# Bursts that end in 128 columns, and a load slot held at the start: a hybrid decoder layer on one core

## The chip, the core and the metric

The kernel runs on one NeuronCore of a Trainium2 chip. The metric is the device time of one launch in microseconds (us), the median over the runs; smaller is better. Profiles are of one execution each. TensorE (PE, its weight loads PEld) multiplies, VectorE (DVE) and ScalarE (ACT) work elementwise, GpSimd (POOL) does small work, SyncE (SP) issues most of the DMAs. A wait is a semaphore that another engine or a DMA raises.

## What is computed

One layer of a decoder on 256 tokens of 2048 channels, in float32:

```python
h = rmsnorm(x, g_mix)
u_pool, q, k, v, q_idx, k_idx, w_idx = split(h @ w_in)
pool_out = pool_mixer(u_pool, w_pool, pool_scale)    # trailing means of 2, 4, 8, 16 tokens
attn_out = dsa_attention(q, k, v, q_idx, k_idx, w_idx, rel_bias)
    # 16 index heads score the causal keys, the best 64 stay; 8 heads of 128 attend
x = x + concat(pool_out, attn_out) @ w_out
x = x + conv_ffn(rmsnorm(x, g_ffn), w_up, conv_w, conv_b, w_down)   # 2048 -> 2 x 5632 -> 2048
x = x + (p @ w_ple_proj) * sigmoid(rmsnorm(x, g_ple) @ w_ple_gate)
return rmsnorm(x, g_final)
```

## The kernel before

Every weight comes through `unit` (L74): a DMA of up to 552 KB on SP into a raw tile of the pool `wraw`, which has four slots; then ACT casts it to a high part (L87, type float32r) and DVE subtracts that from the raw tile, which gives the low part (L88). The raw slot is free when DVE is through. The two parts stand in one of three w tiles. Activations are kept the same way, high and low beside each other.

A product is therefore made of several on TensorE. `cm_matmul` (L143), by far the most frequent, takes each 128 x 128 block of weights twice: the high part against high and low activations, 512 columns (L147), and the low part against the high activations, 256 columns (L148). This pair is most of the kernel: query, key and pool projections, the output projection, the up- and down-projections of the ConvFFN. `tm_matmul` (L167) has the activations as the stationary operand and makes three products for each block (L174, L175, L176).

The stages follow each other in this order. First the input stage (`with ExitStack() as c1`). Its loop over 16 K tiles (L227) multiplies values and index keys: a K tile is 1104 columns of weights, which K tile 0 loads in two units of 368 and 736 columns; six products are made for each of three thirds, 18 a tile. Ahead of the loads stand those of xT, one K tile (128 KB) or two (256 KB) at a time (L230); the first K tile of x comes with the parameters (L93). Then come the pairs for the index queries, q and k, and the pool group, and between them, in bursts, other products: `score` (L305, index scores, float32r, 128 and 256 columns for the two token blocks), the relative bias (L338), `logits` (L388, plain float32, two passes each), the transposes of the softmax (L434 to L436), `attend` (L440, plain float32), and the pool maps (L483). After that the output projection (`out_unit`, L514), the ConvFFN (L535 on), the embedding stage (L584 on) and the stores.

No order is written out by hand. The program is traced, a planner with its own model of times then orders the instructions of each engine, and waits are added where data or a slot need them. A load whose slot isn't free by the planner's times lets later instructions of SP past it, and a burst of other products can land between any two instructions of a pair. `in_order` keeps a few DMAs at their places. At most eight of SP's DMAs are under way: each further one also waits for the landing of the eighth before it. `rstd_rows` (L136) puts four passes of 128 columns (L139) just ahead of the ConvFFN's pairs.

Of the kernel before, what the change touches and what calls it, by code (L numbers as in the profile page):

```python
# [10 lines left out]
F32 = mybir.dt.float32  # L11
# [7 lines left out]
P = 128  # L19
S = 256  # L20
# [14 lines left out]
UNIT = 3 * NVK  # L35
# [15 lines left out]
def layer(ctx: ExitStack, tc: tile.TileContext, a: dict):  # L51
    nc = tc.nc
    in_order = tc.keep_in_program_order
    V, A, T, G = nc.vector, nc.scalar, nc.tensor, nc.gpsimd
# [11 lines left out]
    wraw = ctx.enter_context(tc.tile_pool(name="wraw", bufs=4))  # L66
# [2 lines left out]
    acc = ctx.enter_context(tc.tile_pool(name="acc", bufs=4, space=PSUM))  # L69
    aux = ctx.enter_context(tc.tile_pool(name="aux", bufs=4, space=PSUM))  # L70

    n_units = 0

    def unit(src, n=1024, keep=None, at=(0, LOW)):  # L74

        nonlocal n_units
        raw = wraw.tile([P, UNIT], F32, name="raw")
        nc.sync.dma_start(raw[:, :n], src)
        if keep:
            hi = keep.tile([P, n], F32R, name="hi", bufs=5)  # L80
            lo = keep.tile([P, n], F32R, name="lo", bufs=5)
        else:
            w = wsp[n_units % 3].tile([P, SLOT], F32R, name="w")
            n_units += 1
            h0, l0 = at if n <= 1024 else (0, UNIT)
            hi, lo = w[:, h0:h0 + n], w[:, l0:l0 + n]
        A.copy(hi, raw[:, :n])  # L87
        V.tensor_sub(lo, raw[:, :n], hi.bitcast(F32))  # L88
        return hi, lo
# [117 lines left out]
    with ExitStack() as c1:  # L207
# [8 lines left out]
        qk = ar.tile([P, 2 * NH, S], F32, name="qk", tag="qkA")  # L216
# [10 lines left out]
        for kt in range(KT):  # L227
            if kt == 1 or (kt and kt % 2 == 0):
                k1 = kt + 1 if kt == 1 else kt + 2
                nc.sync.dma_start(xt[:, kt:k1, :], a["xT"][:, kt:k1, :])  # L230
            cuts = (0, NVK, 3 * NVK) if kt == 0 else (0, 3 * NVK)
            ws = [unit(a["w_first"][kt][:, c0:c1], c1 - c0) for c0, c1 in zip(cuts, cuts[1:])]
            split(hT[:, kt, :S], hT[:, kt, S:],
                  xt[:, kt, :] if kt else prm[:, C_CONV:],
                  prm[:, C_GMIX + kt:C_GMIX + kt + 1])
            for n in range(3):
                i = sum(n * NVK >= c for c in cuts) - 1
                tm_matmul(pvk[n], *ws[i], hT, (kt,), kt == 0, kt == KT - 1, n=NVK,
                          w0=n * NVK - cuts[i])
            if kt == 3:  # L240
                in_order(nc.sync.dma_start(ident, a["ident"]))
            if kt == 5:
                in_order(nc.sync.dma_start(xt[:, 0:1, :], a["xT"][:, 0:1, :]))
            if kt >= 7 and kt < 15:
                square(kt - 7)
# [59 lines left out]
        def score(j, qr):  # L305
            pds = [aux.tile([P, 512], F32, name="ps") for _ in range(2)]
            for e in range(2):
                for t, (o, n) in enumerate(((0, P), (P, S))):
                    q = qr[:, e, t * P:(t + 1) * P]
                    T.matmul(pds[e][:, o:o + n], q, kr[:, :n], start=True, stop=False)  # L310
                    T.matmul(pds[e][:, o:o + n], q, kr[:, S:S + n], start=False, stop=True)  # L311
            for e in range(2):
                h = 2 * j + e
                rl = ar.tile([P, 384], F32, name="rl", bufs=2)
                A.activation(rl, pds[e][:, :384], AF.Relu, scale=1.0 / 32.0)
                for t in range(2):
                    src = s0[t] if h == 0 else sc[t]
                    V.scalar_tensor_tensor(sc[t], rl[:, :P] if t == 0 else rl[:, P:],
                                           wx[:, t, h:h + 1], src, op0=OP.mult, op1=OP.add)
# [68 lines left out]
        def logits(t, h0):  # L388
            n = P * (t + 1)
            hb = 512 // n  # L390
            pl = aux.tile([P, 512], F32, name="ps")
            for h in range(h0, h0 + hb):
                T.matmul(pl[:, (h - h0) * n:(h - h0 + 1) * n],  # L393
                         qk[:, 2 * h, t * P:(t + 1) * P], qk[:, 2 * h + 1, :n],
                         start=True, stop=True)
            hs = slice(h0, h0 + hb)
            V.scalar_tensor_tensor(L[t][:, hs, :], pl.rearrange("p (h s) -> p h s", s=n), P ** -0.5,
                                   tb[:, hs, S - n:], op0=OP.mult, op1=OP.add)
# [22 lines left out]
        for j in range(12, 16):  # L421
            qk_tile(j)
            if j >= 14:
                h0 = 4 * (j - 14)
# [15 lines left out]
        def attend(h, pt):  # L440
            po = aux.tile([P, 512], F32, name="ps")
            for e in range(2):
                vs = slice((h + e) * P, (h + e + 1) * P)
                T.matmul(po[:, e * S:(e + 1) * S], v[:, 0, vs], pt[:, e, :S],  # L444
                         start=e == 0, stop=False, skip_group_check=True)
                T.matmul(po[:, e * S + P:(e + 1) * S], v[:, 1, vs], pt[:, e, S:],
                         start=False, stop=e == 1, skip_group_check=True)
            po2 = po.rearrange("p (e s) -> p e s", s=S)
            split(catA[:, h:h + 2, :S], catA[:, h:h + 2, S:], po2)
# [316 lines left out]
```

## Time and profile before

| | us |
|---|---|
| median of 3 runs | 1181.37 (1181.3 to 1181.61) |
| the profiled execution | 1181.5 |
| its span, first to last instruction | 1179.7 |
| TensorE busy in the span | 1168.7 |
| VectorE | 855.8 |
| ScalarE | 643.8 |
| GpSimd | 8.9 |

The input stage ends at about 265 us, the output projection at 357, the up-projection at 827 and the down-projection at 1066 us; the last product starts at 1169.7 us. In the rows below times are us from the span's start unless said otherwise. A matmul's row begins when TensorE takes it up; its end is modelled, so its length holds the way through the array too, and rows of neighbours overlap. What a product occupies TensorE for is read from start to start.

### The profile page before, as it was taken

Reading aid. Unit: us, or ns where it says so; the run is one execution under the profiler, and the core shown is the slowest. Engines: PE = TensorE matmul, PEld = TensorE weight load, DVE = VectorE, ACT = ScalarE, POOL = GpSimd, SP = SyncE. Lnnn points to the kernel's source line nnn. Section 1 sums busy time; section 2 is a strip of 40 time slices with the busy share of each in tenths; the row PEclk is TensorE's granted clock in tenths of the full one; section 3 lists DMA queues with packets and bytes.
Section 4 is the critical chain, followed back from the end, with each engine's and each line's share of the span. In section 5 each row is a group of like instructions: output and inputs, shape, how many; then the busy total and the mean of one; then the engine's idle time right before and its main releaser. Section 6 shows DMA issues by size and latency. Waiting matters only on the chain.

```text
span 1179.7 us, 17843 instructions
## 1 busy us (share of the span) xinstructions
PE 1168.7 (99%) x6792; PEld 1035.6 (88%) x6792; DVE 855.8 (73%) x1314; ACT 643.8 (55%) x941; POOL 8.9 (1%) x27
## 2 busy tenths in 40 slices
PE   9999999999999999999999999999999999999996
PEld 9988888898888888888888888888888888888886
DVE  6578977977778888888888888888555555555564
ACT  7466444555546666666665666666444444444563
POOL 0000000000000000000000000000000000000000
PEclk9999999999999999999999999999999999999998
DMA  9656665446565555555555555556666666667662
GB/s 317 211 174 194 242 205 175 163 145 201 193 200 193 190 194 193 195 194 194 194 191 196 193 194 194 192 195 192 195 190 190 194 196 192 193 192 228 190 210 80
DMA packets 67077, 229.09 MB, mean 194 GB/s; under 512 B 7888, under 2 KB 10072, under 8 KB 66864
## 3 DMA queue, kind: packets, MB, share of 16 engines
q1 hardware_dynamic: 63840, 222.04, 58.4%
q10 hardware_dynamic: 2144, 3.28, 0.9%
q0 software_dynamic: 1008, 2.64, 0.6%
q8 instruction: 53, 0.87, 0.3%
q14 instruction: 32, 0.26, 0.1%
HBM read 224.77 MB, written 3.68 MB: 194 GB/s over the span
## 4 chain that ended last, share of the span: by engine, by line
PE 99%; DMA 0%; DVE 0%; ACT 0%; SPq 0%; POOLq 0%; issue 0%; DVEq 0%
PE pa L147 55%; PE pa L148 28%; PE pa L175 3%; PE pa L174 3%; PE pa L176 3%; PE ps L175 1%; PE ps L176 1%; PE ps L174 1%; PE ps L483 0%; PE ps L393 0%; DMA raw<-in_w_first 0%; PE ps L147 0%; PE ps L310 0%; PE ps L311 0%; PE ps L608 0%; PE ps L444 0%
## 5 line engine op out<-in xcount | busy, mean ns | idle before, releaser
L88 DVE TENSOR_TENSOR w<-raw,w 128x1024 fp32r<-128x1024 f32 (+3 forms) x420 | 503.1, 1198 | 216.3 <-ACT w L87 209.8
L147 PE MATMUL pa<-hT,w 128*128 128x512 f32 x1904 | 652.2, 390 | 0.0
L87 ACT CAST w<-raw 128x1024 fp32r<-128x1024 f32 (+3 forms) x420 | 433.3, 1032 | 339.3 <-PE pa L148 249.9
L148 PE MATMUL pa<-hT,w 128*128 128x256 f32 x1904 | 528.7, 278 | 0.0
L147 PEld LDWEIGHTS pa<-hT,w 128*128 128x128 f32 x1904 | 357.3, 188 | 74.7 <-issue 0.6
L148 PEld LDWEIGHTS pa<-hT,w 128*128 128x128 f32 x1904 | 357.9, 188 | 0.3
L147 PE MATMUL pa<-aT,w 128*128 128x512 f32 x704 | 239.4, 389 | 0.0
L148 PE MATMUL pa<-aT,w 128*128 128x256 f32 x704 | 194.3, 276 | 0.0
L147 PEld LDWEIGHTS pa<-aT,w 128*128 128x128 f32 x704 | 132.1, 188 | 27.7
L148 PEld LDWEIGHTS pa<-aT,w 128*128 128x128 f32 x704 | 132.1, 188 | 0.0
L163 ACT COPY eb<-pa 128x256 f32<-128x256 f32 x119 | 44.4, 373 | 140.2 <-PE pa L148 140.1
L164 DVE TENSOR_TENSOR eb<-pa,eb 128x256 f32<-128x256 f32 x119 | 50.3, 423 | 60.8 <-ACT eb L163 60.7
L175 PE MATMUL pa<-w,hT 128*128 128x512 f32 (+2 forms) x178 | 65.0, 365 | 0.0
L176 PE MATMUL pa<-w,hT 128*128 128x512 f32 (+2 forms) x178 | 64.6, 363 | 0.0
L174 PE MATMUL pa<-w,hT 128*128 128x512 f32 (+2 forms) x178 | 58.4, 368 | 0.1
L550 ACT ACTIVATE cv<-ub,cnv 128x256 f32<-128x256 f32 x88 | 52.8, 602 | 0.2
L147 PE MATMUL pa<-catP,w 128*128 128x512 f32 x128 | 45.9, 391 | 0.0
L147 PE MATMUL pa<-catA,w 128*128 128x512 f32 x128 | 45.6, 390 | 0.0
L554 DVE SCALAR_TENSOR_TENSOR cv<-ub,cnv,cv 128x256 f32<-128x256 f32 x88 | 42.6, 485 | 3.0
L552 DVE SCALAR_TENSOR_TENSOR cv<-ub,cnv,cv 128x256 f32<-128x256 f32 x88 | 41.9, 478 | 0.0
L165 DVE TENSOR_TENSOR ub<-eb,rbc 128x256 f32<-128x256 f32 x88 | 37.3, 425 | 2.9
L175 PEld LDWEIGHTS pa<-w,hT 128*128 128x128 f32 x178 | 33.8, 190 | 4.5 <-DVE w L88 0.6
(175 smaller groups left out, 844.7 us busy)
## 6 DMA issues: line engine op xcount, KB each, us to landing
raw<-in_w_up SPq DMA_DIRECT2D x176, 512.0 KB, 4.7
raw<-in_w_down SPq DMA_DIRECT2D x80, 512.0 KB, 4.0
raw<-in_w_qk SPq DMA_DIRECT2D x32, 512.0 KB, 4.1
raw<-in_w_out SPq DMA_DIRECT2D x32, 512.0 KB, 4.2
raw<-in_w_pg SPq DMA_DIRECT2D x32, 512.0 KB, 4.4
raw<-in_w_first SPq DMA_DIRECT2D x15, 552.0 KB, 5.1
raw<-in_w_qi SPq DMA_DIRECT2D x16, 512.0 KB, 3.8
raw<-in_w_u SPq DMA_DIRECT2D x16, 512.0 KB, 3.8
```

The lines of the kernel that those rows point to most:

```text
L87: A.copy(hi, raw[:, :n])
L88: V.tensor_sub(lo, raw[:, :n], hi.bitcast(F32))
L147: T.matmul(ps, hi[:, w], act, start=first and i == 0, stop=False)
L148: T.matmul(ps[:, :S], lo[:, w], act[:, :S], start=False, stop=last and i == len(acts) - 1)
L163: A.copy(b, ps[:, S:])
L164: V.tensor_add(b, ps[:, :S], b)
L174: T.matmul(pss[t][:, :n], xh, hi[:, w], start=first and i == 0, stop=False)
L175: T.matmul(pss[t][:, :n], xh, lo[:, w], start=False, stop=False)
L176: T.matmul(pss[t][:, :n], xl, hi[:, w], start=False, stop=last and i == len(kts) - 1)
L550: A.activation(t, u[:, 2:], AF.Identity, bias=cnv[:, k + 3:k + 4], scale=cnv[:, k + 2:k + 3])
L552: V.scalar_tensor_tensor(t, u[:, 1:S + 1], cnv[:, k + 1:k + 2], t, op0=OP.mult, op1=OP.add)
L554: V.scalar_tensor_tensor(t, u[:, :S], cnv[:, k:k + 1], t, op0=OP.mult, op1=OP.add)
```

## The change

Four edits. In the loop over K tiles, a further tile of the raw pool is allocated behind tile 1's split, and POOL copies two columns of K tile 0's second raw tile into it; nothing reads it. In `score` the second token block (256 columns) goes ahead of the first (128 columns). In `logits` every product is cut into products of 128 columns, which changes the second token block alone. In `attend` the product of 256 columns is cut into two of 128.

```diff
     def unit(src, n=1024, keep=None, at=(0, LOW)):
-        nonlocal n_units
-        raw = wraw.tile([P, UNIT], F32, name="raw")
+        nonlocal n_units, last_raw
+        last_raw = raw = wraw.tile([P, UNIT], F32, name="raw")
...
             split(hT[:, kt, :S], hT[:, kt, S:],
                   xt[:, kt, :] if kt else prm[:, C_CONV:],
                   prm[:, C_GMIX + kt:C_GMIX + kt + 1])
+            if kt == 0:
+                first_raw = last_raw
+            if kt == 1:
+                hold = wraw.tile([P, UNIT], F32, name="raw")
+                G.tensor_copy(hold[:, :2], first_raw[:, :2])
...
         def score(j, qr):
             pds = [aux.tile([P, 512], F32, name="ps") for _ in range(2)]
             for e in range(2):
-                for t, (o, n) in enumerate(((0, P), (P, S))):
+                for t, o, n in ((1, P, S), (0, 0, P)):
...
             for h in range(h0, h0 + hb):
-                T.matmul(pl[:, (h - h0) * n:(h - h0 + 1) * n],
-                         qk[:, 2 * h, t * P:(t + 1) * P], qk[:, 2 * h + 1, :n],
-                         start=True, stop=True)
+                for k0 in range(0, n, P):
+                    c0 = (h - h0) * n + k0
+                    T.matmul(pl[:, c0:c0 + P], qk[:, 2 * h, t * P:(t + 1) * P],
+                             qk[:, 2 * h + 1, k0:k0 + P], start=True, stop=True)
...
                 vs = slice((h + e) * P, (h + e + 1) * P)
-                T.matmul(po[:, e * S:(e + 1) * S], v[:, 0, vs], pt[:, e, :S],
-                         start=e == 0, stop=False, skip_group_check=True)
+                for t in range(2):
+                    ts = slice(t * P, (t + 1) * P)
+                    T.matmul(po[:, e * S + t * P:e * S + (t + 1) * P], v[:, 0, vs], pt[:, e, ts],
+                             start=e + t == 0, stop=False, skip_group_check=True)
```

## Rows read from the trace of the kernel before

**Rows 1.** The page, part 1: engine, busy us (share of span), instructions.

```profile
PE 1168.7 (99%) x6792; PEld 1035.6 (88%) x6792; DVE 855.8 (73%) x1314; ACT 643.8 (55%) x941; POOL 8.9 (1%) x27
```

**Rows 2.** L147 behind the burst at 159.1 us: count, duration ns min/median/max, first and last start.

```profile
L147 PE MATMUL pa<-hT,w x32: 389/389/396, 159.4 to 170.0; 128*128 128x512 f32 x32
```

**Rows 3.** L147 likewise, behind the bursts at 170.2 and 212.7 us.

```profile
L147 PE MATMUL pa<-hT,w x24: 387/394/396, 171.9 to 179.9; 128*128 128x512 f32 x24
...
L147 PE MATMUL pa<-hT,w x39: 387/393/396, 213.7 to 227.0; 128*128 128x512 f32 x39
```

**Rows 4.** L147 likewise: three stretches behind score bursts, one behind the bias.

```profile
L147 PE MATMUL pa<-hT,w x13: 393/396/396, 74.6 to 78.8; 128*128 128x512 f32 x13
...
L147 PE MATMUL pa<-hT,w x16: 389/389/397, 86.6 to 91.7; 128*128 128x512 f32 x16
...
L147 PE MATMUL pa<-hT,w x16: 393/394/396, 106.0 to 111.2; 128*128 128x512 f32 x16
L147 PE MATMUL pa<-hT,w x23: 395/395/396, 120.1 to 127.9; 128*128 128x512 f32 x23
```

**Rows 5.** L147 by windows: length, busy (instructions), granted clock, DMA share, GB/s.

```profile
172.00:180.00 8.00, 8.00 (x24) 1.00 0.53 172
...
364.00:1066.00 702.00, 702.00 (x2066) 1.00 0.61 193
```

**Rows 6.** Timeline of TensorE round a burst of 128 columns: start, length, engine, line.

```profile
158.88 0.39 PE L147 MATMUL pa<-hT,w 128*128 128x512 f32 x1
159.11 0.38 PE L393 MATMUL ps<-qk 128*128 128x128 f32 x2
...
159.45 0.40 PE L147 MATMUL pa<-hT,w 128*128 128x512 f32 x1
```

**Rows 7.** Timeline of TensorE round a burst of 256 columns.

```profile
188.75 0.39 PE L147 MATMUL pa<-hT,w 128*128 128x512 f32 x1
188.98 0.59 PE L393 MATMUL ps<-qk 128*128 128x256 f32 x2
...
189.53 0.39 PE L147 MATMUL pa<-hT,w 128*128 128x512 f32 x1
```

**Rows 8.** Timeline of TensorE in the output projection.

```profile
279.85 0.28 PE L148 MATMUL pa<-catP,w 128*128 128x256 f32 x1
279.97 0.28 PE L148 MATMUL pa<-catA,w 128*128 128x256 f32 x1
```

**Rows 9.** Timeline of SP's issues of loads.

```profile
3.54 1.63 SPq L78 DMA_DIRECT2D raw<-in_w_first  x2
...
7.59 0.33 SPq L78 DMA_DIRECT2D raw<-in_w_first  x1
7.96 3.50 SPq L230 DMA_DIRECT2D xt<-in_xT  x4
```

**Rows 10.** Timeline of DVE: subtractions of K tiles 0 (two parts) and 1; ACT: tile 1's cast.

```profile
4.27 0.54 DVE L88 TENSOR_TENSOR w<-raw,w 128x368 fp32r<-128x368 f32 x1 [0.17 <-ACT w L87]
6.64 0.93 DVE L88 TENSOR_TENSOR w<-raw,w 128x736 fp32r<-128x736 f32 x1 [1.82 <-ACT w L87]
...
8.88 1.31 DVE L88 TENSOR_TENSOR w<-raw,w 128x1104 fp32r<-128x1104 f32 x1 [0.92 <-ACT w L87]
...
7.73 1.12 ACT L87 CAST w<-raw 128x1104 fp32r<-128x1104 f32 x1 [0.71 <-DMA raw<-in_w_first]
```

**Rows 11.** DMA issues at 3.54, 7.59 and 11.13 us: KB, us from issue to landing.

```profile
raw<-in_w_first SPq DMA_DIRECT2D x1, 552.0 KB, 6.2
...
raw<-in_w_first SPq DMA_DIRECT2D x1, 552.0 KB, 6.9
...
xt<-in_xT SPq DMA_DIRECT2D x1, 256.0 KB, 6.1
```

**Rows 12.** TensorE's waits up to 54.6 us (total, times, longest); timeline of K tile 4.

```profile
PEld pa L175 <- DVE w L88: 0.6, 2, 0.3
...
18.40 0.83 PE L174 MATMUL pa<-w,hT 128*128 128x368 f32 x4
```

More of the change, by code (lines that the diff above doesn't have):

```diff
@@ L70, in layer @@
     aux = ctx.enter_context(tc.tile_pool(name="aux", bufs=4, space=PSUM))
-    n_units = 0
+    n_units, last_raw = 0, None
     def unit(src, n=1024, keep=None, at=(0, LOW)):
-        nonlocal n_units
-        raw = wraw.tile([P, UNIT], F32, name="raw")
+        nonlocal n_units, last_raw
+        last_raw = raw = wraw.tile([P, UNIT], F32, name="raw")
         nc.sync.dma_start(raw[:, :n], src)
```

## Prediction

> **What bounds the kernel now.** I read the page first: TensorE is busy for 1168.7 of 1179.7 us [rows 1] and carries nearly all of the chain that ended last, so only three things can move the end: work on TensorE, the spacing of its instructions, or a wait of TensorE for data. Outside the profiled span lie 1181.5 - 1179.7 = 1.8 us, which the change leaves alone; that execution stands 0.13 us above the median of 1181.37.
>
> Then I read TensorE line by line, start to start, since the ends of its products are modelled. Nearly the whole kernel is one pair of instructions: a 512-column product at L147 and a 256-column one at L148. The reader should see that this pair has **two cadences**. In some stretches pairs start 0.340 us apart (start of L147 to the next L147: 10.6 us over 31 intervals, median duration of the instruction 389 ns) [rows 2]; in others 0.350 us apart (8.0 us over 23, 13.3 us over 38, median 393 to 394 ns) [rows 3]. The granted clock is 1.00, the 2.4 GHz level, in both [rows 5], and DVE, ACT and DMA feed both in time, so it is neither the clock nor a stall. A cadence once taken lasts: the 2066 pairs from 364 to 1066 us all run at 702 / 2066 = 0.340 us [rows 5]. It changes where something else is put between the pairs.
>
> So I listed what stands between them. Of plain float32 products (two passes each) four bursts of one 128-column product (136.9, 148.0, 159.1, 183.3 us) came upon the fast cadence and left it fast; rows 6 and the stretch of rows 2 show the third. Two bursts that end in 256 columns (170.2, 189.0 us) came upon the fast one and left the slow one behind [rows 3, 7]. Out of the slow cadence either kind leads only now and then: one of three 128-ended logits bursts (128.5, not 197.8 and 205.9 us) and one of three 256-ended (180.1, not 200.8 and 212.7 us). Score bursts, which end in 256 columns, left fast pairs behind them in two cases of seven [rows 4].
>
> **The change part by part.**
>
> *Logits.* The 8 products of 256 columns at L393 (second token block) become 16 of 128, so each of those bursts ends in 128 columns. If ending in 128 keeps a cadence, the fast one that rules from 128.8 us lives through. Six stretches between 171.9 and 227.0 us are slow now, with 24, 24, 8, 13, 18 and 39 pairs (first and last in rows 3): 126 pairs x 0.010 us = 1.26 us. Bounds: nothing, and 1.26 us. I take all of it, because four of four 128-ended bursts kept the fast cadence while neither of the two 256-ended ones did.
>
> *Scores.* The two blocks change places, nothing is added; bursts end in 128 columns instead of 256. Five slow stretches between 74.6 and 111.2 us hold 77 pairs (first and last in rows 4), 0.77 us. No 128-ended burst of this operand type followed by a pair was seen to settle a cadence; two of seven 256-ended ones already ended fast. Bounds 0 and 0.77 us, plus the 23 pairs behind the bias product, 7.8 us over 22 intervals = 0.355, so up to 23 x 0.015 = 0.35 us [rows 4]. I take half of the first, 0.4 us.
>
> *Price of the splits.* Sixteen products are cut: 8 at L393, 8 at L444. A 128-column one costs 159.45 - 158.88 - 0.34 = 0.23 us [rows 6], a 256-column one 189.53 - 188.75 - 0.35 = 0.43 to 0.44 us [rows 7]; cut in two it is 0.46. That difference of about 0.02 holds what entering a burst costs, which a cut product pays once and not twice. Bounds 0 and 16 x 0.02 = 0.3 us on TensorE, nothing beside it; I take 0.1. At L444 the burst ends in L446's 128 columns before and after, save where it is cut by other work, so I count no cadence there.
>
> The Trainium skill ("TensorE: Matmul & The Clock Gate", section "Back-to-back issue gap") gives a product a spacing set by its own columns, N / 2.4 + 2.5 ns. By it the pair is 768 / 2.4 + 5 = 325 ns whatever came before, and the change would give no cadence back. The trace disagrees in size and in kind: the same pair is 340 and 350 ns at one granted clock. What a rule without memory would make of the time is the first rival below.
>
> *The hold.* The raw pool has four slots: K tile 0 takes two, tile 1 the third, tile 2 now the fourth. The hold takes the fourth, so tile 2's load needs the slot of tile 0's first part, free when DVE's L88 ends at 4.27 + 0.54 = 4.81 us, tile 3 needs that of the second part (7.57 us), tile 4 that of tile 1 (10.19 us) [rows 10]; tile 5 takes the hold's. Now tiles 3, 4 and 5 wait for these three [rows 9], tile 2 for none. From tile 6 on every load again reuses the slot of four allocations before. Queued behind a waiting load on SP are tile 3, then xT loads and the identity. The copy waits on POOL for the DMA of tile 0's second part, which DVE's L88 takes up at 6.64 us at the latest [rows 10]; behind it POOL has nothing that anyone needs before rstd_of (L128), at the end of this stage, so nothing is held up there.
>
> What is it worth? Transfers land in the order of issue. Tile 2 is issued at about 4.0 us (the two issues of 3.54 us) and lands at 3.54 + 6.2 = 9.7 us [rows 9, 11]: it spends most of that behind others, so issuing it at 4.84 moves its landing little. The loads ahead of it are ahead already, so I see no gain; the two waits of TensorE for a low part, 0.6 us together [rows 12], bound one. Tile 4 decides. It is issued now at 7.59 us, ahead of four xT loads [rows 9], and lands at 14.5 [rows 11]. The planner puts those four ahead of the load that needs tile 1's slot; if that is now tile 4, four loads of 256 KB land first. The bytes up to then are the same, so tile 4 lands when the last of the four does now: issued by 11.46, a little after 11.1 us, it lands 6.1 us later, at 17.2 [rows 9, 11]. That is (17.2 - 14.5) / 4 = 0.68 us for each of them. Cast and subtraction take 1.12 + 1.31 us [rows 10]: 19.65. TensorE starts tile 4 at 18.40 and spends 6 x 0.167 = 1.0 on the products that don't need the low part [rows 12]: 19.40. It stalls for 0.25 us. Bounds -0.6, and +2.7 us (the last rival, where tile 2 is late too). I take +0.25: nearest to what SP's order shows.
>
> Sum: -1.26 - 0.4 + 0.1 + 0.25 = -1.3 us; 1181.5 - 1.3 = 1180.2 for the execution profiled, **1180.1** by the median.
>
> **The rivals.**
>
> *No steering.* The cadence after a burst is chance, and 128 columns don't hold it; or the hold delays nothing that was not queued anyway. Then 0.1 to 0.3 us is added: 1181.4 + 0.3 = **1181.7**. For it: the slow cadence survived two 128-ended logits bursts. Against it: four of four held the fast one.
>
> *All fast.* All score stretches and the bias product's turn fast too, and the start doesn't stall: 1.26 + 0.77 + 0.35 = 2.4, with part of the 0.6 us of rows 12 on top 2.6: **1178.8**.
>
> *The long stage goes slow* (the other side). FFN's 2066 pairs inherit the cadence of the output projection, which turns fast at 280.1 us, where the planner let two L148 follow each other [rows 8]. That is an accident of its order, and new instructions before it shift its times. If the swap goes, the pairs from 280 to 357 us stay slow, the bursts at 356.9 and 362.7 us rarely repair it, and every pair of FFN then costs 0.010 us more: 2066 x 0.010 = 20.7, with some 220 pairs of the projection (75 / 0.340) 22.9 us: about **1204**, or 1202 if only FFN goes. It decides at the first pair behind 363 us. For it: nothing in 700 us of FFN would reset a cadence, nor did anything in the 39 slow pairs up to 227 us. Against it: the projection's own code is untouched, and the burst ahead of FFN (L139) is of 128-column products, which kept the fast cadence before.
>
> *The start starves.* The planner lets all six xT loads past tile 2: 6 x 0.68 = 4 us later, landing at 13.7 us; TensorE wants tile 2 six microseconds before tile 4 (18 products of 0.167 us a tile), its high part at 12.4 and its low part by 13.4 us. With 2.4 us of casting that is a stall of 2.7 us: 1181.4 - 1.26 - 0.4 + 0.1 + 2.7 = **1182.5**, or 1184 without the cadences.
>
> **How the numbers follow.** Forecast (1180.1, between 1179.0 and 1181.4) 0.43; no steering 0.20; all fast 0.14; long stage slow 0.15; start starved 0.08. A change of 0.2% is 2.4 us, about what can be told from none here. Faster than that (below 1179.0) needs all fast: 0.15. Slower (above 1183.7): the long stage and the worst of the start, 0.18. Within: 0.67. The range takes in all but the long stage and half of the starved start: 1178.4 to 1183.4. The forecast's own is 1179.0 to 1181.6.
>
> **What would show it.** Right: L147 in the six stretches between 172 and 227 us with a median of 389 ns and starts 0.340 apart; L393's bursts taking the same time; tile 2's issue at 4.84 us, tile 3's at 7.6, four xT issues ahead of tile 4, one wait of TensorE near 19.4 us. Wrong: 393 to 395 ns in stretches behind bursts that end in 128 columns; a wait ahead of tile 2 at 12.4 us; above all 393 ns or more at L147 behind 363 us, which makes the prediction wrong by twenty times its gain.

## The result, and the profile after

The changed kernel takes **1188.35 us** (median of 4 runs, 1187.99 to 1189.63) against 1181.48 beside it: a ratio of 1.0058, 95% interval 1.0046 to 1.0071. The profiled execution took 1187.99 us, its span is 1186.2 us, 6.5 more than before. The forecast was 1180.1, and 1188.35 lies outside the range.

I first laid the two timelines of TensorE beside each other, by the start of the same product in both:

| start of | before, us | after, us | lost up to there |
|---|---|---|---|
| first pair behind the loop over K tiles | 54.61 | 54.65 | 0.0 |
| first logits burst | 128.49 | 128.82 | 0.3 |
| fifth logits burst | 170.22 | 171.70 | 1.5 |
| 129th product of the output projection | 282.47 | 286.61 | 4.1 |
| first product of the up-projection | 347.75 | 353.81 | 6.1 |
| first product of the down-projection | 827.40 | 833.88 | 6.5 |
| last product | 1169.66 | 1176.15 | 6.5 |

The loop over K tiles loses nothing, and the ConvFFN loses nothing behind its first pairs. Everything lies between 70 and 370 us. TensorE's page row says that it is busy for 4.5 us more:

```profile
PE 1173.2 (99%) x6824; PEld 1038.8 (88%) x6824; DVE 855.6 (72%) x1314; ACT 643.6 (54%) x941; POOL 9.1 (1%) x28
```

The duration of L147 shows most of it. Rows of the changed kernel by line and stretch (count, ns min/median/max, first and last start):

```profile
L147 PE MATMUL pa<-hT,w x13: 389/389/443, 74.5 to 78.7; 128*128 128x512 f32 x13
...
L147 PE MATMUL pa<-hT,w x16: 395/396/443, 79.9 to 85.2; 128*128 128x512 f32 x16
...
L147 PE MATMUL pa<-hT,w x118: 393/393/396, 129.2 to 170.8; 128*128 128x512 f32 x118
...
L147 PE MATMUL pa<-hT,w x24: 395/396/396, 172.7 to 180.8; 128*128 128x512 f32 x24
...
L147 PE MATMUL pa<-catP,w x108: 393/394/396, 278.9 to 353.5; 128*128 128x512 f32 x108
...
L147 PE MATMUL pa<-hT,w x1362: 389/389/389, 370.8 to 833.5; 128*128 128x512 f32 x195
L147 PE MATMUL pa<-aT,w x704: 389/389/389, 833.9 to 1072.9; 128*128 128x512 f32 x176
```

The 119 pairs from 129 to 171 us ran at 389 ns before (the last of their stretches is rows 2) and now run at 393. The stretch behind 171.7 us, which was to turn fast, has gone from 394 ns [rows 3] to 396. Behind six of the seven score bursts [rows 4] stands 396; behind the first (74.5 us) the pairs have turned fast, 389. The output projection has gone from 389 to 394. Only the ConvFFN keeps 389.

Starts show that there are three cadences, not two: 340 ns a pair; 350 (intervals of 348 and 352, or 349 and 351, in turn; the prediction called it slow); and **353.5** (350 and 357 in turn), which before stood behind the bias product [rows 4] and, briefly, at a few other places (8 pairs from 277.1 us). It now follows six score bursts and the burst at 171.7 us, and behind the bias product stands 350.

The projection is slow from one place on. Before, two L148 that followed each other came upon 0.3535 at 280 us and turned it fast [rows 8]; after, they come upon the fast cadence and turn it slow:

```profile
278.32 0.28 PE L148 MATMUL pa<-catP,w 128*128 128x256 f32 x1
278.44 0.28 PE L148 MATMUL pa<-catA,w 128*128 128x256 f32 x1
```

The second loss is a stall that did not exist before. Timeline of TensorE, then of ACT, changed kernel (start, length, engine, line; in brackets the idle time before and what ended it):

```profile
233.93 1.59 PE L492 MATMUL ps<-plr,w 128*128 128x256 f32 x11
235.35 0.61 PE L453 MATMUL ps<-pt,v 128*128 128x128 f32 x4
...
237.01 0.49 PE L147 MATMUL pa<-hT,w 128*128 128x512 f32 x1 [0.83 <-ACT w L87]
238.28 0.39 PE L148 MATMUL pa<-hT,w 128*128 128x256 f32 x1 [0.78 <-DVE w L88]
...
235.55 0.48 ACT L115 ACTIVATE catP<-ps,prm 128x256 fp32r<-128x256 f32 x1 [1.07 <-PE ps L492]
235.92 1.04 ACT L87 CAST w<-raw 128x1024 fp32r<-128x1024 f32 x1
```

TensorE wants the next unit right behind the attend burst, some 0.7 us after the pool map's products (L492) end. The cast of that unit (L87) starts only at 235.92, and the subtraction follows it; its load, issued at 219.21, had landed at 222.9. Before, transposes, two attend bursts and another pool map stood between those products and the pair.

The hold came out otherwise than forecast. SP's issues after, beside rows 9, then POOL's copy, then from the list of waits what SP's loads waited for:

```profile
3.06 0.91 SPq L230 DMA_DIRECT2D xt<-in_xT  x2
4.70 1.58 SPq L78 DMA_DIRECT2D raw<-in_w_first  x2
6.33 0.42 SPq L247 DMA_DIRECT2D ident<-in_ident  x1
6.81 0.44 SPq L230 DMA_DIRECT2D xt<-in_xT  x1
7.50 0.33 SPq L78 DMA_DIRECT2D raw<-in_w_first  x1
7.87 3.15 SPq L230 DMA_DIRECT2D xt<-in_xT  x4
...
5.74 0.18 POOL L241 COPY raw<-raw 128x2 f32<-128x2 f32 x1 [4.34 <-DMA raw<-in_w_first]
...
SPq L78 <- POOL raw L241: 0.8, 1, 0.8
```

One more xT load goes ahead of tile 2 (4.70). POOL is through with the held slot at 5.92 us, and the next load, tile 3's, takes that slot. So tile 4 (the load at 7.50) needs the slot of tile 0's second part, as before, and the four xT loads stay behind it.

### The profile page after: what moved, and what is told of

It reads as the page before. It is cut to its first block, busy times and chain, and to the rows that moved or that the text cites. A ratio compares the mean times of both kernels' runs of the same rounds, so it can differ in the third digit from the quotient of the medians.

```text
span 1186.2 us, 17907 instructions
## 1 busy us (share of the span) xinstructions
PE 1173.2 (99%) x6824; PEld 1038.8 (88%) x6824; DVE 855.6 (72%) x1314; ACT 643.6 (54%) x941; POOL 9.1 (1%) x28
## 4 chain that ended last, share of the span: by engine, by line
PE 97%; DVE 1%; DMA 0%; issue 0%; ACT 0%; SPq 0%; POOLq 0%; DVEq 0%; ACTq 0%
PE pa L147 55%; PE pa L148 28%; PE pa L175 3%; PE pa L176 3%; PE pa L174 3%; PE ps L175 1%; PE ps L176 1%; PE ps L174 1%; DVE w L88 0%; PE ps L401 0%; DMA raw<-in_w_first 0%; PE ps L492 0%; PE ps L147 0%; PE ps L317 0%; PE ps L617 0%
## 5 line engine op out<-in xcount | busy, mean ns | idle before, releaser
L147 PE MATMUL pa<-hT,w 128*128 128x512 f32 x1904 | 655.3, 391 | 0.8 <-ACT w L87 0.8
L87 ACT CAST w<-raw 128x1024 fp32r<-128x1024 f32 (+3 forms) x420 | 433.2, 1032 | 337.6 <-PE pa L148 244.4
L148 PE MATMUL pa<-hT,w 128*128 128x256 f32 x1904 | 529.4, 278 | 0.8 <-DVE w L88 0.8
L147 PEld LDWEIGHTS pa<-hT,w 128*128 128x128 f32 x1904 | 357.5, 188 | 76.9 <-ACT w L87 1.0
L148 PEld LDWEIGHTS pa<-hT,w 128*128 128x128 f32 x1904 | 358.1, 188 | 1.2 <-DVE w L88 1.1
L147 PE MATMUL pa<-aT,w 128*128 128x512 f32 x704 | 239.4, 389 | 0.0
L148 PE MATMUL pa<-aT,w 128*128 128x256 f32 x704 | 194.3, 276 | 0.0
L147 PEld LDWEIGHTS pa<-aT,w 128*128 128x128 f32 x704 | 132.2, 188 | 27.0
L148 PEld LDWEIGHTS pa<-aT,w 128*128 128x128 f32 x704 | 132.2, 188 | 0.0
L147 PE MATMUL pa<-catP,w 128*128 128x512 f32 x128 | 46.8, 395 | 0.0
L147 PE MATMUL pa<-catA,w 128*128 128x512 f32 x128 | 46.6, 394 | 0.0
```

The costliest lines, as they stand in the source:

```text
L147: T.matmul(ps, hi[:, w], act, start=first and i == 0, stop=False)
L148: T.matmul(ps[:, :S], lo[:, w], act[:, :S], start=False, stop=last and i == len(acts) - 1)
```

## The experiments

**One edit at a time.** Each is the kernel before with one of the four edits, as in the diff above.

> The hold alone. On SP it only moves one 256 KB load of xT ahead of K tile 2's load; TensorE's order is that of before. In the changed kernel's trace the input stage ends 0.04 us later than before. If the loss of 6.9 us comes from bursts and from the planner's order behind 54 us (theory A), this kernel stays at 1181.5, within 0.2 us. If the held slot starves the start (theory B), it is slower by 0.5 us or more, with waits of TensorE ahead of 20 us.

Measured: 1181.79 us, ratio 1.000 (0.9991 to 1.0009). TensorE's order is that of before, SP's is that of the changed kernel. The hold costs nothing.

> The reordered score bursts alone. TensorE's order changes only between 72 and 119 us. Theory A (a burst hands on or changes the cadence of the pairs, and 128 columns at its end keep nothing): the pairs behind the score bursts run at 0.350 to 0.357 us, those from 129 to 170 us at 0.350 instead of 0.340 (119 pairs, +1.2 us), together +1.5 to +2.5 us: 1183 to 1184. The theory of the forecast: up to 0.8 us faster, 1180.7. Price of splits alone (theory C): no change, since nothing is split here.

Measured: 1183.24 us, ratio 1.001 (1.0001 to 1.002). Behind six of the seven score bursts stands 0.3535. Behind the bias product and then behind the first logits bursts:

```profile
L147 PE MATMUL pa<-hT,w x25: 393/396/496, 120.5 to 129.1; 128*128 128x512 f32 x25
...
L147 PE MATMUL pa<-hT,w x119: 393/394/397, 128.7 to 170.9; 128*128 128x512 f32 x119
```

Logits are uncut here. What decides is the stretch behind the bias product: it ran at 0.3535 before [rows 4], and the single 128-column product at 128.5 us turned that fast; it now runs at 0.350, and the same product (129.3 us) keeps it. The three behind it keep what they find.

> The cut logits products alone. Theory A: the price of the cut on TensorE is about 0.4 us (13 more bursts and 16 more passes); most of the rest is order: the planner moves bursts, transposes and a few pairs between 170 and 290 us, and if TensorE then waits near 237 us for a cast of ACT (2 us in the changed kernel) and the output projection runs at 0.350 us (+2.2 us), this kernel is at 1183.5 to 1186. Theory C (the cut itself costs): +0.4 us, 1181.9, with no wait and a fast projection.

Measured: 1186.81 us, ratio 1.0044 (1.0029 to 1.0059): the dearest edit. The stall of about 2 us is there (ACT's split waits 1.44 us for the pool map at 234.80), and the projection is slow from 277 to 362 us. The planner has spread the cut products over more bursts, 15 in the changed kernel for 12. The first burst with cut products, four of 128 columns at 170.67 us, comes upon the fast cadence, since no score edit stands ahead of it, and leaves the slow one; rows ahead of it and behind it:

```profile
L147 PE MATMUL pa<-hT,w x32: 389/389/396, 159.9 to 170.4; 128*128 128x512 f32 x32
...
L147 PE MATMUL pa<-hT,w x24: 393/395/396, 171.7 to 179.7; 128*128 128x512 f32 x24
```

> The cut products of attend alone. Its order in the output projection is that of the changed kernel. Theory A: the projection's pairs run at 0.350 us up to 363 us (+2.2 us) while the stretches up to 228 us are those of before: 1183.5 to 1184, more if the wait near 237 us is here too. Theory C: 16 more passes of 0.11 us against 16 passes that are shorter by as much, +0.1 us: 1181.6.

Measured: 1184.58 us, ratio 1.0022 (1.0012 to 1.0031). No stall; the two L148 now at 274.95 us leave the projection slow, 67.08 us from its 129th product to its last, as in the changed kernel, for 65.17 before. So the projection's 2.2 us (up to the ConvFFN) come with either cut, and are paid once where both are made.

**Does the last product of a burst decide?** The kernel before, with one more product in the burst just ahead of the ConvFFN, its result unused: one of 256 columns, or two of 128.

```diff
+        for o in range(0, S, tail):      # tail = 256 or 128
+            T.matmul(ps[:, S + o:S + o + tail], r[:, 0:1].to_broadcast([P, P]), xt[:, 0, o:o + tail],
+                     start=True, stop=True)
```

> The kernel before, with one more float32 product of 256 columns behind the four 128-column passes just ahead of the ConvFFN; its result goes to an unused part of a PSUM tile. TensorE's order is otherwise that of before. If the last burst sets a cadence that then lasts, as rows 5 and rows 8 of the document suggest, the ConvFFN's 2066 pairs run either at 0.340 (1181.9) or at 0.350 us (1202). A burst that ends in 256 columns upon the fast cadence left the slow one behind both times before: so 1202. If a cadence doesn't last on its own: 1181.9 (0.43 us for the product).

> As the run beside it, but the extra 256 columns are two products of 128, the same work. If ending in 128 keeps the fast cadence: 0.340 us a pair behind it, 1181.9. If what a burst leaves is a matter of its length and phase and not of the columns of its last product, either of 1181.9 and 1202 can come.

Measured: 1182.2 (ratio 1.0002, 0.999 to 1.0013) and 1181.85 us (1.0001, 0.9989 to 1.0012). The ConvFFN runs at 0.340 behind both, first with the 256 columns, then with the two of 128 (L150 is L147 there):

```profile
L150 PE MATMUL pa<-hT,w x1346: 389/389/389, 370.8 to 828.1; 128*128 128x512 f32 x193
...
L150 PE MATMUL pa<-hT,w x1347: 389/389/389, 370.8 to 828.5; 128*128 128x512 f32 x193
```

What this burst ends in does not decide.

**The stall.** First theory: ACT's order, since the split (L115) that waits for L492 stands ahead of the cast. The split is put behind the cast:

```diff
-                    pool_map(*done.pop())
+                    owed.append(pool_map(*done.pop(), later=True))   # its two splits
...
+                    with tc.issue_after(casts[-1]):                   # behind the sixth w_u tile's cast
+                        owed.pop()()
```

> The changed kernel, with the two splits of the third pool map (ACT's Copy into catP) put behind one weight cast, that of the second half of the sixth tile of w_u, which in the changed kernel stands behind them on ACT. Nothing is added or left out. Theory A (ACT's order makes the stall: the split waits for the pool map's products and holds up a cast whose load landed long before): the two waits of 0.8 us each at 236 to 238 us go, and what hangs on them: 1188.35 - 2.0 = 1186.3 us. Rival B (the load, DVE or the PSUM tile is late by itself): the waits stay, 1188.4 us. Rival C (the wait moves to the split's reader): one wait of about as much behind catP, 1188.4 us.

Measured: 1188.25 us. The theory fell. ACT's cast, now first, waits just as long, and for the same products:

```profile
236.78 1.04 ACT L89 CAST w<-raw 128x1024 fp32r<-128x1024 f32 x1 [1.07 <-PE ps L494]
```

(L494 there is the changed kernel's L492.) A cast reads raw and writes a w tile; PE can only hold up the second. Three w tiles go round, and the pool map's weights occupy one: the third unit behind them must wait for the last product that reads them. So the second theory: the tile, which the pool map's products hold until 0.7 us before it is needed, with cast and subtraction still to come. The test gives those weights memory of their own.

```diff
-            hi, lo = unit(a["w_pool"][g], 512)
+            hi, lo = unit(a["w_pool"][g], 512, own=wp)   # two tiles that are free in this stage
```

> The changed kernel, with the pool maps' weights cast into a tile of their own (the memory of two others that are free then) instead of one of the three w tiles; the w tiles rotate as before, so the load that follows three units behind a pool map's finds its slot free. The planner is left to order the rest and moves some bursts between 200 and 285 us. Theory A (the stall at 236 to 238 us was the cast's wait for the w tile that the pool map's products were still reading, 1.07 us of it on PE): no wait of TensorE of over 0.3 us between 225 and 245 us, 1188.35 - 2.0 = 1186.3 us, with up to 2 us either way if a stretch changes its cadence. Rival B (TensorE outruns the casts there, the bursts being shorter than ACT's and DVE's work for one unit, whatever the slot): the waits stay or move to the next unit, 1188.4 us.

Measured: 1186.1 us, 2.25 less, as the second theory has it. TensorE's window from 230 to 245 us (length, busy and count for PE, PEld, DVE, ACT, POOL, then clock, DMA share, GB/s), changed kernel and then this one:

```profile
230.00:245.00 15.00, 13.39 (x90) 11.88 (x89) 12.59 (x24) 8.93 (x19) 0.25 (x2) 1.00 0.46 144
```

```profile
230.00:245.00 15.00, 15.00 (x102) 13.70 (x101) 13.33 (x25) 11.02 (x21) 0.25 (x2) 1.00 0.51 161
```

The 1.6 us of idle time are gone. The planner also moved bursts in this kernel, so the 2.25 is not the tile's alone, and this run by itself does not part the tile from the order. The cast's wait for L494, above, does.

**The projection.** The changed kernel with two float32 products of 128 columns in the projection, 3 us behind the two L148:

```diff
             T.matmul(ps, hi[:, w], act, start=first and i == 0, stop=False)
+            if i == 7 and extra:      # extra: two products of 128 columns, result unused
```

> The changed kernel, with two float32 products of 128 columns (four passes, as L139 has) put between the two products of one pair of the output projection, some 3 us behind the place where two 256-column products follow each other; their result is not used. Theory A (the projection is slower than before by its cadence alone, and four passes of 128 columns turn a slow cadence fast, as L139 did three times of three): from there to 363 us starts are 0.340 apart, some 230 pairs x 0.010 = 2.3 less and 0.45 more: 1188.35 - 1.85 = 1186.5 us. Rival B (128-column products keep whatever cadence they find, L139's repair had another cause): starts stay 0.350 apart, 1188.35 + 0.45 = 1188.8 us. Rival C (the projection is slow by its loads or evictions): starts mixed, 1188.8 us.

Measured: the profiled execution 1186.41 us, 1.6 less than the changed kernel's, as theory A has it; from the projection's 129th product to its last 65.17 us for 67.08 (65.17 before):

```profile
L147 PE MATMUL pa<-catP,w x104: 389/389/390, 282.5 to 352.2; 128*128 128x512 f32 x104
```

The median of the four runs is 1187.65. The other three were not profiled; what may lie between is in the next run.

**The scores undone.** The changed kernel with the old `score`.

> The changed kernel with the old order of blocks in the score bursts (first the 128-column products, then the 256-column ones); hold and both cuts as in the change. Theory A (the reordered score burst leaves the slowest cadence, 0.3535, and a slow one up to 171 us): what the score edit did alone comes off, 1188.35 - 1.2 = 1187.1 us, or 1186.7 by the traces, with 0.340 apart from 129 to 171 us as before; the stall at 236 us and the slow projection stay. Rival B (the edits' costs don't add, the planner's later orders depend on the earlier ones): the later stages come out otherwise, 1184 to 1189 us.

Measured: 1188.36 us, no gain in the median. Up to the fifth logits burst the timeline is that of before again (170.24 us), 1.5 us less than after. Then the gain is lost at one place, behind the same stall:

```profile
234.00:237.00 3.00, 1.39 (x8) 0.89 (x8) 3.00 (x7) 2.27 (x4) 0.12 (x1) 0.98 0.55 198
237.00:239.00 2.00, 2.00 (x8) 1.71 (x8) 1.39 (x3) 0.57 (x1) 0.12 (x1) 0.50 0.60 188
```

The granted clock falls to 0.50, the 1.2 GHz level, until 240 us; five pairs take 0.64 us each, 1.5 us in all. In the changed kernel's own profile the same stall left the clock at 1.00. The Trainium skill ("TensorE: Matmul & The Clock Gate", section "HAM oscillation — how this bites in real kernels") tells of a kernel that paid for longer waits of TensorE twice, by the wait and by a colder clock behind it; this trace shows the same behind two waits of 0.8 us, that of the changed kernel does not. A stall there thus costs 2 or 3.5 us, and medians of kernels that have it say less than their traces. Of this kernel's four runs the one with the highest mean clock (0.997) took 1187.43 us. Of the four runs of the kernel with two products in the projection, the two with the lowest mean clock (0.995 and 0.996) took 1188.4 and 1187.95 us, the two others (0.997, 0.998) 1187.36 and 1186.41.

**How long a cadence lasts.** The kernel before with one unused float32 product of 256 columns early in the up-projection; then with two of 128 some 344 pairs later as well.

```diff
             up_pair(c, [cm_tile(a["w_up"], 2 * c + e) for e in range(2)])
+            if c == 1:
+                T.matmul(px[:, :256], aT[:, 1, :P].bitcast(F32), xt[:, 0, :256], start=True, stop=True)
+            if c == 12:               # second kernel only: two of 128 columns
```

> The kernel before, with one unused float32 product of 256 columns put between the two products of one pair at the beginning of the up-projection (behind its second pair of tiles). Every other instruction keeps its place. Theory A (a cadence once taken lasts, and one such product turned the fast one slow in six of six cases of the attention stage): some 2025 pairs up to 1066 us at 0.350 instead of 0.340 and the product's 0.44: 1181.4 + 20.3 + 0.4 = 1202 us. Rival B (the slow cadence belongs to the attention stage and the projection, to their loads or to DVE and ACT, and cannot last in the up-projection): 1181.8 us.

> As the run with one product of 256 columns, and some 344 pairs later two unused float32 products of 128 columns between the two products of a pair. Theory A (four passes of 128 columns turn the slow cadence fast): 344 x 0.010 = 3.4 and 0.9 for the products: 1181.4 + 4.3 = 1185.7 us, with 0.350 between the two places and 0.340 behind. Rival B (what repairs is not the burst's make but the moment): slow to the end of the down-projection, 1181.4 + 20.3 + 0.9 = 1202.6 us.

Measured: **1201.92** (ratio 1.0172, 1.0155 to 1.0189) and 1186.21 us (1.004, 1.0025 to 1.0055). One product of 0.44 us costs 20 us, because nothing behind it turns the cadence back:

```profile
L147 PE MATMUL pa<-hT,w x1311: 393/396/396, 382.9 to 841.4; 128*128 128x512 f32 x188
L147 PE MATMUL pa<-aT,w x704: 393/394/396, 841.8 to 1087.8; 128*128 128x512 f32 x176
```

All other instructions stand where they stood, DVE and ACT do the same work (858.6 and 643.4 us busy for 855.8 and 643.8), and the clock is 1.00. No other engine shows a cause: the cadence is a state of TensorE's own stream.

**What the next cadence depends on.** 35 unused bursts in the up-projection of the kernel before, 32 pairs apart, each right behind an L147.

> The kernel before, with 35 unused bursts in the up-projection, one behind each second pair of tiles (32 pairs apart), each right behind a 512-column product, every other instruction in its place. Bursts of float32: one, two, three or four products of 128 columns (2, 4, 6, 8 passes), one or two of 256; of float32r: one of 256 or of 512. Each is set behind the fast cadence (after a burst of two products of 128) and behind the slow one (after that and one of 256). Theory A (the cadence after a burst follows from the cadence before it and the burst's make, at one place of the pair): the 14 bursts of two 128s all leave 0.340 and the 8 of one 256 that follow them all 0.350, and one 128 keeps what it finds, in both tries. Rival B (by chance, or by the time at which it falls): equal bursts come out unequally. The prediction's rule (what ends in 128 keeps the fast one) would hold for one to four 128s behind the fast cadence.

Measured: 1206.45 us (one run). Theory A as written fell: equal bursts left different cadences. But the trace sorts them. Within the slow cadence longer and shorter pairs alternate, and it matters on whose turn the burst falls. Cadence that the burst left, us per pair (times seen):

| burst | found 0.340 | found 0.350, longer pair's turn | shorter pair's turn | found 0.3535 |
|---|---|---|---|---|
| one of 128 | | 0.350 (2) | | |
| two of 128 | 0.350 (6) | **0.340 (3)** | **0.3535 (5)** | |
| three of 128 | 0.340 (1) | 0.350 (1) | | |
| four of 128 | 0.350 (1) | | | 0.350 (1) |
| one of 256 | 0.350 (1) | 0.340 (5) | | 0.350 (3) |
| two of 256 | 0.340 (2) | | | |
| float32r, one of 256 | 0.350 (1) | 0.340 (1) | | |
| float32r, one of 512 | 0.340 (1) | | | 0.350 (1) |

Each box holds one outcome, though many were seen only once. Three of the bursts of two 128s by their rows behind them: found 0.340, found 0.350 on the shorter pair's turn, found it on the longer's:

```profile
L150 PE MATMUL pa<-hT,w x32: 393/395/396, 391.0 to 401.8; 128*128 128x512 f32 x32
...
L150 PE MATMUL pa<-hT,w x32: 395/396/396, 414.1 to 425.0; 128*128 128x512 f32 x32
...
L150 PE MATMUL pa<-hT,w x32: 389/389/398, 437.4 to 448.0; 128*128 128x512 f32 x32
```

Two products of 128 behind the fast cadence, which the prediction's rule calls harmless, leave the slow one six times of six.

The kernels' own logits bursts agree, counted over the traces of all 18 kernels where they fall right behind an L147. One product of 128 kept 0.340 (61 of 61) and 0.350 on either turn (50 of 50) and turned 0.3535 into 0.340 (21 of 21). Two of 128 left 0.350 behind 0.340 (4 of 4), 0.340 on the longer pair's turn (2 of 2) and 0.3535 on the shorter's (5 of 5).

The table does not reach all bursts. L139's two products at 60.5 us stand behind an L148. All 18 kernels have the same 361 products up to the 25th behind them, TensorE waits for nothing in that stretch, and the pairs come upon 0.340. Yet the burst left 0.350 in 14 profiles, 0.3535 in three and 0.340 in one. The pairs behind it in the kernel before, with the hold alone, and with the scores undone:

```profile
L147 PE MATMUL pa<-hT,w x12: 393/396/468, 61.1 to 65.0; 128*128 128x512 f32 x12
...
L147 PE MATMUL pa<-hT,w x12: 395/396/468, 60.8 to 64.8; 128*128 128x512 f32 x12
...
L147 PE MATMUL pa<-hT,w x12: 389/389/473, 61.2 to 65.0; 128*128 128x512 f32 x12
```

What decides there is open.

**Three causes undone at once**, in the changed kernel: the pool maps' own memory, the old `score`, and the two products in the projection.

> The changed kernel with three causes taken away at once: the pool maps' weights in a tile of their own (no stall at 236 us), the old order of blocks in the score bursts (no slow cadence up to 171 us), and two unused products of 128 columns in the output projection (slow cadence turned fast there). Hold and both cuts stay. Theory A (these three make nearly all of the 6.9 us, and they add): 1186.1 - 1.4 - 1.85 = 1182.9 us, 1.3 to 1.5 above before. Rival B (another loss takes their place): 1185 us or more.

Measured: 1185.55 us (ratio 1.0032, 1.002 to 1.0045), 2.7 more than expected. There is no stall and nothing slow up to 170 us, but the two products left 0.3535 instead of 0.340. They had fallen on the shorter pair's turn. If the table is right, one pair decides; so the same burst was moved by one pair and nothing else, one pair earlier here, and one pair later in the up-projection of the kernel that had been turned slow and back.

> As the run with three causes taken away, with the two unused products in the output projection one pair earlier; nothing else moves. Theory A (the slow cadence alternates, 348 and 352 ns or 351 and 349 ns, and two 128s turn it fast behind the longer half, whose 512-column product lasts 234 to 235 ns to its successor, and to 0.3535 behind the shorter half, of 231 to 233; there they fell on 233): one pair earlier they fall on the longer half, starts are 0.340 apart up to 361 us, 240 pairs x 0.0135 = 3.2 less: 1185.55 - 3.2 = 1182.3 us. Rival B (the place does not matter, the state left by the earlier stages does): 0.3535 again, 1185.5 us.

> As the run that turned the up-projection slow by one product of 256 columns and fast again by two of 128 some 344 pairs later, with these two one pair later; nothing else moves. Theory A (there they fell behind the longer half, 234 ns; one pair later they fall on the shorter, 231): they leave 0.3535 instead of 0.340 for the 1670 pairs left, 1670 x 0.0135 = 22.6 more: 1186.2 + 22.6 = 1208.8 us. Rival B (two 128s turn the slow cadence fast wherever they fall): 1186.2 us. Rival C (they keep it, 0.350): 1186.2 + 16.7 = 1202.9 us.

Measured: **1182.78** (ratio 1.0006, 0.9997 to 1.0016) and **1208.67 us** (1.0226, 1.0209 to 1.0243), for 1182.3 and 1208.8 expected. The projection, first with the burst on the shorter pair's turn, then one pair earlier:

```profile
L149 PE MATMUL pa<-catP,w x104: 395/396/397, 278.4 to 350.8; 128*128 128x512 f32 x104
```

```profile
L149 PE MATMUL pa<-catP,w x105: 388/389/397, 278.3 to 349.1; 128*128 128x512 f32 x105
```

And the up-projection, first as it was, then one pair later: two L147 and the burst from the timeline, and the stretch behind. The turn is seen in the rows' lengths: the L147 ahead of the burst is the longer one (0.40) in the first and the shorter (0.39) in the second.

```profile
501.99 0.39 PE L147 MATMUL pa<-hT,w 128*128 128x512 f32 x1
...
502.33 0.40 PE L147 MATMUL pa<-hT,w 128*128 128x512 f32 x1
502.57 0.61 PE L581 MATMUL ps<-xt,aT 128*128 128x128 f32 x4
...
L147 PE MATMUL pa<-hT,w x966: 389/389/390, 503.8 to 831.9; 128*128 128x512 f32 x194
```

```profile
502.40 0.40 PE L147 MATMUL pa<-hT,w 128*128 128x512 f32 x1
...
502.75 0.39 PE L147 MATMUL pa<-hT,w 128*128 128x512 f32 x1
502.98 0.61 PE L578 MATMUL ps<-xt,aT 128*128 128x128 f32 x4
...
L147 PE MATMUL pa<-hT,w x966: 394/396/397, 503.9 to 844.9; 128*128 128x512 f32 x194
```

Moving two products by 0.35 us moves the end by 22.5 us. And with three causes gone, hold and both cuts still in, the kernel is back within 0.7 us of before: they account for 6.2 of the 6.9 us.

No version beat both kernels by more than can be told. What is slow in the kernel before is worth 2.4 us by the prediction's own count [rows 3, 4], in stretches of 8 to 39 pairs, and a burst that repairs one costs 0.45.

## Why the prediction was wrong, step by step

*What bounds the kernel.* Right: nearly all of the loss is TensorE's own, by cadence and by a wait. Two cadences were one too few; the 0.355 behind the bias was the third, taken for a feature of that product. The 325 ns set against the trace go by a formula which the Trainium skill ("TensorE: Matmul & The Clock Gate", section "Back-to-back issue gap") gives for a single product by itself and not for a stream of them.

*Logits, -1.26: the step that failed.* "If ending in 128 keeps a cadence" was read from four bursts of one single product, which do keep it, the slow one too, and laid upon bursts of two to four products, which are another thing: behind 0.340, two of 128 left 0.350 six times of six, and with the logits edit alone four of 128 did the same at 170.67 us. The last product's width was the one feature I looked at; length and turn decide. None of the 126 pairs counted turned fast: the 24 behind 171.7 us came out at 0.3535, because their burst found the slow cadence, and the others stayed at 0.350, so -1.26 measured +0.1. And "the fast one that rules from 128.8 us" was taken as given, though the score edit stands ahead of it: those 119 pairs cost 1.15 us. The prediction had the sign of this before it: one 128-ended burst, at 128.5 us, had led out of a slow cadence, and that cadence was the third.

*Scores, -0.4: the wrong sign.* +0.3 up to 128.5 us, and the 1.15 us above. Nothing in the trace showed a burst that ends in float32r products of 128; the lower bound was set at no loss without a reason that excluded one.

*Price of the splits, +0.1.* By starts attend's passes fit it (4.95 us for 4.73 where they alone are cut), but for the stall at their end. The logits took 4.08 us for 3.70, +0.4 where the bound was 0.3 for both. The planner broke 12 bursts into 15; that each entry costs would explain it but was not tested by itself.

*The hold, +0.25.* Measured 0. The step that failed is who gets the held slot: the prediction gave it to tile 5, and tile 1's slot to tile 4. The copy gave it back at 5.92 us and tile 3's load took it, so tile 4 did not move behind the four xT loads.

*The order taken as fixed.* Here lies the largest term, which the sum does not have. With the logits cut the planner put the pool map's products right ahead of the unit that needs their weight tile, 2.0 us; the kernel with that cut alone has this stall, the one with attend's alone has not. And with either cut the projection goes slow, 2.2 us. The prediction saw that new instructions shift the planner's order, but used it for one rival alone, and of L444 it said that no cadence was to be counted: its cut alone cost 2.5 us, by the projection. With the scores' 0.3 and 1.15 and the logits' 0.4 these two make 6.1 of the 6.5 us between the two traces.

*The rival "no steering".* Right that ending in 128 columns holds nothing; but it called the cadence chance and added no more than the splits' 0.1 to 0.3, where by the table the next cadence mostly follows from the burst, and can be the worse one.

*The rival "the long stage goes slow".* Its first half happened: the two L148 no longer turn the projection fast, 2.2 us. Its second did not: L139's burst found the slow cadence and turned it fast, here and in the four other kernels where it found it. Why is not shown. The table's boxes are of products of one stationary operand, and the two signs of the turn disagree here: the last whole pair ahead of the burst was a longer one (352 ns), so the turn was the shorter's, but L147 took the 235 ns to its successor that go with the longer's. On the shorter's turn the probes' two products of 128 left 0.3535, which over the ConvFFN would have cost over 20 us; that it went well was no merit of the sum. That rival's price was right, 20 us when the up-projection was turned slow, and its condition was only half understood: it said that a 128-column burst rarely repairs.

## What to carry to other kernels

Before counting on a pattern in a trace, look whether all its cases are of one make: a rule read from single products need not hold for bursts. In a kernel whose order a planner writes, an added instruction is priced with the order that it upsets; check above all which tile's last reader moves close to the tile's next writer. And where one pair of instructions fills hundreds of microseconds, measure its start-to-start time in every stage, for a state that some earlier burst has left can be worth more than the edit.

## What was not expected of the hardware

- The same pair of products runs at 340, 350 or 353.5 ns at a granted clock of 1.00, for as long as nothing comes between: 2015 pairs in the run with one added product.
- Which one follows a burst of float32 products right behind an L147 is no chance. In 350 ns the pairs alternate; two unused products of 128 columns left 340 on the longer pair's turn (six of six with the other runs) and 353.5 on the shorter's (seven of seven). Behind an L148 one and the same burst left all three.
- The columns are not all of it: ahead of the ConvFFN L139's two products of 128, whose stationary operands differ, left 340 behind 340 in the kernel before, where the probes left 350. What the state is inside TensorE was not found.
- A stall of 2 us was followed by 3 us at half clock in one profile and by none in another.
